# The attention mask of a hybrid block: written into the sigmoids' diagonal blocks by GpSimd, or added to the scores by VectorE

## The chip, the cores and the metric

The kernel runs on one core of one Trainium2 chip. The metric is the device time of one execution in microseconds (us); the median of three runs stands for a kernel. Every duration below comes from one profiled execution of the kernel before.

## The reference, cut to what matters

The whole block is a norm of x, ten projections, a stick-breaking attention of 8 heads, a retention of 4 heads, gates, and an output projection. Only the attention is touched. For a query t and a key s < t its weight is the sigmoid of the score times the product of (1 - sigmoid) over the keys between s and t; keys at and behind t count nothing:

```python
mask = kpos[None, :] < qpos[:, None]
log_keep = jnp.where(mask, jax.nn.log_sigmoid(-z), 0.0)
suffix = lax.cumsum(log_keep, axis=3, reverse=True) - log_keep
w = jnp.where(mask, jnp.exp(jax.nn.log_sigmoid(z) + suffix), 0.0)
return jnp.einsum('bhqk,bhkd->bhqd', w.astype(v.dtype), v)
```

The sequence has 512 tokens, a head is 128 wide, and the work is cut into blocks of 128 queries, so only the 128x128 block on the diagonal needs a mask.

## The kernel before, in words

**Dense stages.** Twenty-six dense products of 512x1024 by 1024x512 make up most of the work: the q/k groups qk0 to qk3 (two heads each), v0 and v1, the gates, the retention's projections, the two branch products and the final product. Each float32 operand is split into a high and a low part (`split`, L115 and L116: ScalarE copies the high part, VectorE subtracts to get the low one), and each product is three matmuls (`mm3`, L86). A dense stage takes four PSUM banks out of five (`ps_mm`) and walks over eight slices of 128 rows of the weights, which arrive by DMA in pairs and are split on the way.

**Side work.** Attention and retention are generators. After every two of a dense stage's tile products `work.step()` lets the generator at the front issue its next piece, so TensorE's order interleaves them. Matmuls, transposes and loads keep the order in which the program is written (`tc.keep_in_program_order`). The other engines' instructions are put in an order by a scheduler when the program is built, and each engine then works through its own list strictly in that order: one that waits holds up all behind it.

**A block of the attention** is a pair (head, query block), written (h, b) here. `scores` (L373 to L391) forms z in a side PSUM bank of TensorE, lets VectorE add the mask to the diagonal block (L382), lets ScalarE write keep = sigmoid(-z) (L385) and beta = sigmoid(z) (L386) into SBUF, and lets VectorE run the product of keep from the right as a scan (L387) and multiply it into beta (L391). `weights`, two blocks later, transposes beta on TensorE into a side bank pw (L89) and splits it into the pair wT (L115 on ScalarE, L116 on VectorE). `values`, three blocks after a head's last scores, multiplies all of wT with v into po (L86).

**GpSimd** has little to do. For each q/k group it raises the mean squares to -1/2 (L190, `rr`), multiplies this by the token norm (L302) and scales the four raw 128x512 tiles by it (L304, `qraw`). These are transposed much later by the generator `post`. When the groups qk0, qk1 and qk3 end, no scan of the attention is due; the group qk2 ends while heads 2 and 3 are in work, because qk2 follows directly on qk1.

The lines that the prediction speaks of:

```python
nc.vector.tensor_add(z[:, ts], z[:, ts], neg_mask)
nc.scalar.activation(keep[:, :n], z[:, :n], AF.Sigmoid, scale=-sc)
nc.scalar.activation(bt[:, :n], z[:, :n], AF.Sigmoid, scale=sc)
```

Of the kernel before, what the change touches and what calls it, by code (L numbers as in the profile page):

```python
# [7 lines left out]
F32 = mybir.dt.float32  # L8
F32R = mybir.dt.float32r
AF = mybir.ActivationFunctionType  # L10
ALU = mybir.AluOpType

P = 128
# [5 lines left out]
HD = 128  # L19
RH = 4  # L20
EPS = 1e-6
MASKED = -1e30

C_Q, C_K, C_V, C_G = 0, 1024, 2048, 3072
C_RQ, C_RK, C_RV, C_RG = 4096, 5120, 6144, 7168
# [42 lines left out]
def hybrid_block(ctx, tc, x, x_t, vecs, w_in, w_a, w_b, w_o, cos_t, sin_t, decay, out):  # L68
    nc = tc.nc
    PSUM = bass.MemoryType.PSUM  # L70

    const = ctx.enter_context(tc.tile_pool(name="const", bufs=1))
# [15 lines left out]
    def transpose(*a):  # L88
        tc.keep_in_program_order(nc.tensor.transpose(*a))  # L89

    def mm3(ps, a, b, first, last):

        matmul(ps, a[0], b[0], start=first, stop=False)
        matmul(ps, a[0], b[1], start=False, stop=False)
        matmul(ps, a[1], b[0], start=False, stop=last)

    def side_psum(name):
        return ps_a.tile([P, S], F32, tag="a", name=name)

    def T_tile(name, dtype=F32R):  # L100
        return big.tile([P, 4, S], dtype, tag="T", bufs=4, name=name)
# [4 lines left out]
    def O_pair(name):  # L106
        return [big.tile([P, S], F32R, tag="O", bufs=16, name=f"{name}_{q}") for q in range(2)]
# [3 lines left out]
    def tmp_tile(name):  # L111
        return tmp.tile([P, S], F32, tag="tmp", name=name)

    def split(hi, lo, src):
        nc.scalar.copy(hi, src)  # L115
        nc.vector.tensor_sub(lo, src, f32(hi))  # L116
# [54 lines left out]
    for j in range(N_IDLE):  # L171
# [1 line left out]

    ident = const.tile([P, P], F32, name="ident")
    make_identity(nc, ident)
    neg_mask = const.tile([P, P], F32, name="neg_mask")
    nc.gpsimd.memset(neg_mask, 0.0)
    nc.gpsimd.affine_select(
        out=neg_mask, in_=neg_mask, pattern=[[-1, P]], base=0, channel_multiplier=1,
        compare_op=ALU.is_gt, fill=MASKED,  # L180
    )
    for t in wT_pair:
        nc.vector.tensor_copy(t[:, NT - 1, (NT - 2) * P : (NT - 1) * P], zero.broadcast_to([P, P]))
    m_half = const.tile([P, M_ROOM], F32, name="m_half")[:, :16]
# [185 lines left out]
    def attention(heads, ready, v, gates):  # L370

        blocks = [(h, b) for h in heads for b in range(NT)]
        beta = {}  # L373

        def scores(h, b):
            hi, lo = qk_parts[h // 2]
            a, n = h % 2, (b + 1) * P
            ts = slice(b * P, n)
            z = side_psum(f"z{h}_{b}")
            m = max(n, 256)  # L380
            mm3(z[:, :m], (hi[:, a, ts], lo[:, a, ts]), (hi[:, 2 + a, :m], lo[:, 2 + a, :m]), True, True)
            nc.vector.tensor_add(z[:, ts], z[:, ts], neg_mask)  # L382
            bt = tmp.tile([P, S], F32, tag="beta", bufs=3, name=f"beta{h}_{b}")
            keep = tmp.tile([P, S], F32, tag="keep", bufs=2, name=f"keep{h}_{b}")
            nc.scalar.activation(keep[:, :n], z[:, :n], AF.Sigmoid, scale=-sc)  # L385
            nc.scalar.activation(bt[:, :n], z[:, :n], AF.Sigmoid, scale=sc)  # L386
            nc.vector.tensor_tensor_scan(  # L387
                keep[:, :n][:, ::-1], keep[:, :n][:, ::-1], zero.broadcast_to([P, n]), 1.0,
                op0=ALU.mult, op1=ALU.add,
            )  # L390
            nc.vector.tensor_mul(bt[:, : n - 1], bt[:, : n - 1], keep[:, 1:n])  # L391
            beta[h, b] = bt

        def weights(h, b):
            hi, lo = wT_pair
            bt = beta.pop((h, b))
            pw = side_psum(f"pw{h}_{b}").rearrange("p (i t) -> p i t", t=P)
            for i in range(b + 1):
                transpose(pw[:, i, :], bt[:, i * P : (i + 1) * P], ident)
            ts = slice(b * P, (b + 1) * P)  # L400
            split(hi[:, : b + 1, ts], lo[:, : b + 1, ts], pw[:, : b + 1, :])

        def values(h):
            hi, lo = wT_pair
            po = side_psum(f"po{h}")
            cs = slice((h % 4) * P, (h % 4 + 1) * P)
            vv = v()
            for i in range(NT):
                t0 = min(i, NT - 2) * P
                mm3(po[:, t0:], (vv[i][0][:, cs], vv[i][1][:, cs]), (hi[:, i, t0:], lo[:, i, t0:]),  # L410
                    i == 0, i == NT - 1)
            o = tmp_tile(f"oa{h}")
            nc.vector.tensor_mul(o, po, gates()[h % 4])
            oa[h] = O_pair(f"oa{h}")
            split(oa[h][0], oa[h][1], o)

        for n in range(len(blocks) + 3):
            if n < len(blocks):
                scores(*blocks[n])
                yield W_Z  # L420
            if n >= 3 and blocks[n - 3][1] == NT - 1:
                while not ready():
                    yield 1
                values(blocks[n - 3][0])
                yield W_Z
            if 2 <= n < len(blocks) + 2:
                weights(*blocks[n - 2])
                yield W_W
# [111 lines left out]
    for g in range(2):  # L540
        m = gate_group(f"ma{g}", C_MA + S * g, V_BM + 4 * g)
        ps = dense(f"pa{g}", branch_act(oa), w_a, ((S * g, S),), False)
        t = T_tile(f"pa{g}", F32)
# [26 lines left out]
    for g in range(2):  # L570
# [3 lines left out]
        for j in range(4):  # L574
            t = tmp_tile(f"mg{g}_{j}")
# [75 lines left out]
```

## Time and profile before

| what | value |
|---|---|
| median of three runs | 662.97 us (661.91 to 663.33) |
| the profiled execution | 663.5 us |
| its span, first to last instruction | 661.7 us |
| TensorE (PE) busy | 656.0 us, 99% of the span |
| VectorE (DVE), ScalarE (ACT), GpSimd (POOL) busy | 375.5, 260.4, 50.7 us |
| granted TensorE clock | full, mean 1.000 |

The span is the trace's own time; the execution's time has 1.8 us more around it. PEld is TensorE's loading of weights, which overlaps its matmuls. A row of a timeline gives the start in us, the duration in us, the engine, the line, the operation and its output and inputs; where the engine stood idle before, a bracket gives for how long and what ended the wait. Tile names there leave out buffer numbers and digits, so `keep`, `beta`, `z`, `pw` and `po` stand for all blocks and heads.

### The profile page before, as it was taken

What the parts mean: (1) busy time and instruction counts of PE and PEld (TensorE: products, weight loads), DVE (VectorE), ACT (ScalarE), POOL (GpSimd) and SP (SyncE); (2) the same over time, 40 slices, a digit from 0 to 9 for tenths busy, and PEclk for the clock granted to TensorE, in tenths of its full rate; (3) what the DMA queues carried; (4) which work ended last, traced back from release to release, by engine and by line L of the source; (5) the groups of instructions that cost most, each with busy time, mean ns of one, the idle gap of its engine ahead of it and who ended that gap; (6) DMA issues with size and microseconds to landing.
All of it is one profiled execution on the core that took longest, in us unless ns stands there. A gap on an engine that the chain in (4) does not pass through costs nothing.

```text
span 661.7 us, 7982 instructions
## 1 busy us (share of the span) xinstructions
PE 656.0 (99%) x3097; PEld 545.4 (82%) x3097; DVE 375.5 (57%) x560; ACT 260.4 (39%) x417; POOL 50.7 (8%) x50
## 2 busy tenths in 40 slices
PE   9999999999999999999999999999999999999997
PEld 6878888888888888888888888888888888888886
DVE  6356864587497477632344764844862953544632
ACT  5744534564354554522312342433433443422310
POOL 0051000340000400000000001001001001000000
PEclk9999999999999999999999999999999999999999
DMA  8533123322322323233223323222323322335441
GB/s 286 194 126 95 64 63 96 96 64 65 95 64 66 95 63 97 64 96 96 95 96 111 96 64 111 85 76 80 97 74 102 96 64 64 96 95 161 158 159 63
DMA packets 42182, 65.02 MB, mean 98 GB/s; under 512 B 2848, under 2 KB 19488, under 8 KB 42144
## 3 DMA queue, kind: packets, MB, share of 16 engines
q1 hardware_dynamic: 41424, 63.45, 30.9%
q10 hardware_dynamic: 720, 1.07, 0.4%
q8 instruction: 24, 0.39, 0.2%
q14 instruction: 14, 0.11, 0.1%
HBM read 62.41 MB, written 2.10 MB: 97 GB/s over the span
## 4 chain that ended last, share of the span: by engine, by line
PE 93%; DMA 2%; DVE 1%; ACT 1%; POOL 1%; issue 1%; SPq 0%; DVEq 0%; POOLq 0%
PE rqk_ps L86 13%; PE qk_ps L86 10%; PE sg_ps L86 7%; PE ma_ps L86 7%; PE rv_ps L86 7%; PE mb_ps L86 7%; PE rg_ps L86 7%; PE fin_ps L86 7%; PE pb_ps L86 7%; PE pa_ps L86 7%; PE v_ps L86 5%; PE po L86 2%; PE rz L86 2%; PE z L86 2%; PE ro L86 2%; PE pw L89 1%
## 5 line engine op out<-in xcount | busy, mean ns | idle before, releaser
L86 PE MATMUL qk_ps<-qk_hi,xT_hi 128*128 128x512 f32 x128 | 51.4, 410 | 0.0
L86 PE MATMUL rqk_ps<-xT_hi,rqk_hi 128*128 128x512 f32 x128 | 50.5, 394 | 0.0
L86 PE MATMUL rqk_ps<-xT_hi,rqk_lo 128*128 128x512 f32 x128 | 50.0, 390 | 0.0
L86 PE MATMUL rqk_ps<-xT_lo,rqk_hi 128*128 128x512 f32 x128 | 49.9, 390 | 0.0
L86 PE MATMUL qk_ps<-qk_hi,xT_lo 128*128 128x512 f32 x128 | 49.1, 391 | 0.0
L86 PE MATMUL qk_ps<-qk_lo,xT_hi 128*128 128x512 f32 x128 | 49.0, 391 | 0.0
L86 PE MATMUL pb_ps<-ob,pb_hi 128*128 128x512 f32 x128 | 39.4, 389 | 0.0
L86 PE MATMUL pa_ps<-oa,pa_hi 128*128 128x512 f32 x128 | 39.4, 389 | 0.0
L116 DVE TENSOR_TENSOR rqk_lo<-rqk_raw,rqk_hi 128x1024 fp32r<-128x1024 f32 x16 | 20.8, 1299 | 23.9 <-ACT rqk_hi L115 23.9
L387 DVE TENSOR_TENSOR_SCAN keep<-keep,zero 128x128 f32<-128x128 f32 (+3 forms) x32 | 27.1, 847 | 7.3 <-ACT keep L385 7.3
L86 PEld LDWEIGHTS qk_ps<-qk_hi,xT_hi 128*128 128x128 f32 x128 | 24.5, 192 | 5.3 <-ACT xT_hi L160 0.9
L86 PEld LDWEIGHTS qk_ps<-qk_hi,xT_lo 128*128 128x128 f32 x128 | 24.0, 188 | 5.2
L190 POOL TENSOR_TENSOR rrr<-ms,m_half 128x4 f32<-128x4 f32 x4 | 4.0, 1007 | 316.3 <-DVE ms L189 316.3
L86 PEld LDWEIGHTS rqk_ps<-xT_hi,rqk_lo 128*128 128x128 f32 x128 | 24.0, 188 | 5.1
L86 PEld LDWEIGHTS pa_ps<-oa,pa_hi 128*128 128x128 f32 x128 | 24.0, 188 | 5.0
L86 PEld LDWEIGHTS pb_ps<-ob,pb_hi 128*128 128x128 f32 x128 | 24.0, 188 | 5.0
L86 PEld LDWEIGHTS rqk_ps<-xT_hi,rqk_hi 128*128 128x128 f32 x128 | 24.1, 188 | 4.7
L86 PEld LDWEIGHTS rqk_ps<-xT_lo,rqk_hi 128*128 128x128 f32 x128 | 24.1, 188 | 4.6
L86 PEld LDWEIGHTS qk_ps<-qk_lo,xT_hi 128*128 128x128 f32 x128 | 24.3, 190 | 4.3
L115 ACT CAST rqk_hi<-rqk_raw 128x1024 fp32r<-128x1024 f32 x16 | 16.8, 1051 | 25.8 <-PE rqk_ps L86 16.5
L86 PE MATMUL v_ps<-v_hi,xT_hi 128*128 128x512 f32 x64 | 26.1, 408 | 0.0
L86 PE MATMUL sg_ps<-xT_hi,sg_hi 128*128 128x512 f32 x64 | 25.9, 404 | 0.0
(185 smaller groups left out, 1701.2 us busy)
## 6 DMA issues: line engine op xcount, KB each, us to landing
rqk_raw<-in_w_in SPq DMA_DIRECT2D x32, 256.0 KB, 2.9
qk_raw<-in_w_in SPq DMA_DIRECT2D x28, 256.0 KB, 3.0
v_raw<-in_w_in SPq DMA_DIRECT2D x8, 512.0 KB, 3.7
sg_raw<-in_w_in SPq DMA_DIRECT2D x8, 512.0 KB, 3.7
rv_raw<-in_w_in SPq DMA_DIRECT2D x8, 512.0 KB, 3.6
ma_raw<-in_w_in SPq DMA_DIRECT2D x8, 512.0 KB, 3.6
pa_raw<-in_w_a SPq DMA_DIRECT2D x8, 512.0 KB, 3.9
rg_raw<-in_w_in SPq DMA_DIRECT2D x8, 512.0 KB, 3.7
```

The costliest lines, as they stand in the source:

```text
L86: tc.keep_in_program_order(nc.tensor.matmul(*a, **k))
L89: tc.keep_in_program_order(nc.tensor.transpose(*a))
L115: nc.scalar.copy(hi, src)
L116: nc.vector.tensor_sub(lo, src, f32(hi))
L190: nc.gpsimd.tensor_tensor(dst, t[:, :width], m_half[:, :width], op=ALU.pow)
L387: nc.vector.tensor_tensor_scan(keep[:, :n][:, ::-1], keep[:, :n][:, ::-1], zero.broadcast_to([P, n]), 1.0, op0=ALU.mult, op1=ALU.add,)
```

## The change

The table of -1e30 (`neg_mask`) and the 32 additions of it to z in PSUM are gone. In their place GpSimd writes into the diagonal 128x128 block of each of the two sigmoids in SBUF: 1.0 into keep and 0.0 into beta where the key isn't earlier than the query. Each of the 32 blocks of the attention so has two selects (64 in all). The scan now waits for the select on keep, the product for the select on beta. Below the removed lines every line number is one lower up to L176, and from L178 on the function `earlier_keys` holds the selects (L178 for all 64); `scores` has its scan at L388 and its product at L392.

```diff
-MASKED = -1e30
...
-    neg_mask = const.tile([P, P], F32, name="neg_mask")
-    nc.gpsimd.memset(neg_mask, 0.0)
-    nc.gpsimd.affine_select(
-        out=neg_mask, in_=neg_mask, pattern=[[-1, P]], base=0, channel_multiplier=1,
-        compare_op=ALU.is_gt, fill=MASKED,
-    )
+
+    def earlier_keys(t, fill):
+
+        nc.gpsimd.affine_select(
+            out=t, in_=t, pattern=[[-1, P]], base=0, channel_multiplier=1, compare_op=ALU.is_gt, fill=fill,
+        )
...
-            nc.vector.tensor_add(z[:, ts], z[:, ts], neg_mask)
...
             nc.scalar.activation(keep[:, :n], z[:, :n], AF.Sigmoid, scale=-sc)
+            earlier_keys(keep[:, ts], 1.0)
             nc.scalar.activation(bt[:, :n], z[:, :n], AF.Sigmoid, scale=sc)
+            earlier_keys(bt[:, ts], 0.0)
```

TensorE's list and SyncE's are the same in both programs. Those of GpSimd, VectorE and ScalarE differ. In the listings the first digit of `keep_`, `beta_`, `z_` and `pw_` is the query block b, the last number is a buffer; the scan is listed as SCALAR_TENSOR_TENSOR.

GpSimd's list in the changed program, where the group qk2 ends; `keep_3_1294` is block (2,3), the last of head 2, and `keep_0_1325` is block (3,0), the first of head 3:

```order
L178 AFFINE_SELECT keep_3_1294<-keep_3_1294 128x128
L178 AFFINE_SELECT beta_3_1293<-beta_3_1293 128x128
L190 TENSOR_TENSOR rr_1253<-ms,m_half 128x16
L302 TENSOR_TENSOR rr_1253<-rr_1253,rx 128x16
L304 TENSOR_TENSOR qraw_0_1233<-qraw_0_1233,rr_1253 128x512
L304 TENSOR_TENSOR qraw_1_1235<-qraw_1_1235,rr_1253 128x512
L304 TENSOR_TENSOR qraw_2_1237<-qraw_2_1237,rr_1253 128x512
L304 TENSOR_TENSOR qraw_3_1239<-qraw_3_1239,rr_1253 128x512
L178 AFFINE_SELECT keep_0_1325<-keep_0_1325 128x128
L178 AFFINE_SELECT beta_0_1324<-beta_0_1324 128x128
L178 AFFINE_SELECT keep_1_1363<-keep_1_1363 128x128
```

Before, the six instructions of the group's norm stood alone here; now the selects of (3,0) and all that follow stand behind them, those of (2,3) ahead.

VectorE's list at the same place, before (`pw_3_1341` is the transposed block (2,3), `ms` what the group's norm waits for):

```order
L189 TENSOR_SCALAR ms<-ss_1204 128x16
L116 TENSOR_TENSOR v_lo_1368<-v_raw_1365,v_hi_1367 128x1024
L387 SCALAR_TENSOR_TENSOR keep_0_1295<-keep_0_1295,zero 128x128
L391 TENSOR_TENSOR beta_0_1294<-beta_0_1294,keep_0_1295 128x127
L116 TENSOR_TENSOR wT_77<-pw_2_1312,wT_76 128x3x128
L382 TENSOR_TENSOR z_1_1324<-z_1_1324,neg_mask 128x128
L387 SCALAR_TENSOR_TENSOR keep_1_1330<-keep_1_1330,zero 128x256
L391 TENSOR_TENSOR beta_1_1329<-beta_1_1329,keep_1_1330 128x255
L116 TENSOR_TENSOR wT_77<-pw_3_1341,wT_76 128x4x128
```

And in the changed program (`pw_3_1378` is block (2,3)):

```order
L189 TENSOR_SCALAR ms<-ss_1232 128x16
L115 TENSOR_TENSOR v_lo_1408<-v_raw_1405,v_hi_1407 128x1024
L115 TENSOR_TENSOR wT_77<-pw_2_1346,wT_76 128x3x128
L388 SCALAR_TENSOR_TENSOR keep_0_1325<-keep_0_1325,zero 128x128
L392 TENSOR_TENSOR beta_0_1324<-beta_0_1324,keep_0_1325 128x127
L388 SCALAR_TENSOR_TENSOR keep_1_1363<-keep_1_1363,zero 128x256
L392 TENSOR_TENSOR beta_1_1362<-beta_1_1362,keep_1_1363 128x255
L115 TENSOR_TENSOR wT_77<-pw_3_1378,wT_76 128x4x128
```

The subtraction for (2,3) stands behind two scans and two products as before, but these scans now wait for GpSimd.

VectorE's list where the gate group sg1 hands its PSUM banks to qk3, in the changed program (`sg_ps_1557` is the third of sg1's four banks, `keep_2_1744` is block (4,2)):

```order
L354 TENSOR_TENSOR sg_0_1759<-sg_0_1759,sg_s_1767 128x512
L388 SCALAR_TENSOR_TENSOR keep_2_1744<-keep_2_1744,zero 128x384
L349 TENSOR_TENSOR sg_2_1763<-sg_ps_1557,rb 128x512
L392 TENSOR_TENSOR beta_2_1743<-beta_2_1743,keep_2_1744 128x383
L115 TENSOR_TENSOR qk_lo_1855<-qk_raw_1851,qk_hi_1854 128x1024
L349 TENSOR_TENSOR sg_3_1765<-sg_ps_1558,rb 128x512
```

Before, the products that empty the third and fourth bank stood ahead of both the product with `sg_s` and the scan of (4,2); now the third stands behind them.

## Rows read from the trace of the kernel before

**Rows 1.** The page: busy time, share of the span and instructions of each engine.

```profile
PE 656.0 (99%) x3097; PEld 545.4 (82%) x3097; DVE 375.5 (57%) x560; ACT 260.4 (39%) x417; POOL 50.7 (8%) x50
```

**Rows 2.** Waits of TensorE: who for whom; us in total, times, longest.

```profile
PE pi L86 <- DVE idle L169: 1.2, 1, 1.2
PE pqk L89 <- POOL qraw L304: 0.4, 1, 0.4
```

**Rows 3.** The line L382: durations min/median/max in ns, and who waited for it.

```profile
L382 DVE TENSOR_TENSOR z<-z,neg_mask x32: 267/294/300, 59.8 to 265.5; 128x128 f32<-128x128 f32 x32
...
  ACT keep L385: 25.3, 18
```

**Rows 4.** Groups of GpSimd by form: busy us, mean ns of one.

```profile
L178 POOL TENSOR_SCALAR_AFFINE_SELECT neg_mask<-neg_mask 128x128 f32<-128x128 f32 x1 | 0.3, 287 | 0.0
```

**Rows 5.** Timeline of GpSimd, at the ends of the groups qk2 and qk3.

```profile
140.90 3.81 POOL L190 TENSOR_TENSOR rr<-ms,m_half 128x16 f32<-128x16 f32 x1 [18.35 <-DVE ms L189]
144.78 0.22 POOL L302 TENSOR_TENSOR rr<-rr,rx 128x16 f32<-128x16 f32 x1
145.08 5.08 POOL L304 TENSOR_TENSOR qraw<-qraw,rr 128x512 f32<-128x512 f32 x4
224.20 2.90 POOL L190 TENSOR_TENSOR rr<-ms,m_half 128x16 f32<-128x16 f32 x1 [74.04 <-DVE ms L189]
...
227.51 4.04 POOL L304 TENSOR_TENSOR qraw<-qraw,rr 128x512 f32<-128x512 f32 x4
```

**Rows 6.** Timeline of VectorE, 118 to 166 us.

```profile
140.66 0.16 DVE L189 TENSOR_SCALAR ms<-ss 128x16 f32<-128x16 f32 x1
140.73 1.22 DVE L116 TENSOR_TENSOR v_lo<-v_raw,v_hi 128x1024 fp32r<-128x1024 f32 x1
141.87 0.44 DVE L387 TENSOR_TENSOR_SCAN keep<-keep,zero 128x128 f32<-128x128 f32 x1
142.41 0.29 DVE L391 TENSOR_TENSOR beta<-beta,keep 128x127 f32<-128x127 f32 x1
142.62 0.55 DVE L116 TENSOR_TENSOR wT<-pw,wT 128x384 fp32r<-128x384 f32 x1
...
144.06 0.69 DVE L387 TENSOR_TENSOR_SCAN keep<-keep,zero 128x256 f32<-128x256 f32 x1 [0.51 <-ACT keep L385]
144.86 0.42 DVE L391 TENSOR_TENSOR beta<-beta,keep 128x255 f32<-128x255 f32 x1
145.68 0.69 DVE L116 TENSOR_TENSOR wT<-pw,wT 128x512 fp32r<-128x512 f32 x1 [0.40 <-ACT wT L115]
...
149.18 1.79 DVE L387 TENSOR_TENSOR_SCAN keep<-keep,zero 128x384 f32<-128x384 f32 x1
```

**Rows 7.** Timeline of TensorE, 143 to 168 us: the values of head 2.

```profile
148.19 0.63 PE L86 MATMUL po<-wT,v_hi 128*128 128x512 f32 x2
148.66 0.39 PE L86 MATMUL po<-wT,v_lo 128*128 128x512 f32 x1
```

**Rows 8.** Timeline of VectorE, 178 to 208 us: sg1 hands its banks to qk3.

```profile
188.44 1.28 DVE L349 TENSOR_TENSOR sg<-sg_ps,rb 128x512 f32<-128x512 f32 x2
...
190.78 0.95 DVE L387 TENSOR_TENSOR_SCAN keep<-keep,zero 128x384 f32<-128x384 f32 x1
191.65 0.67 DVE L354 TENSOR_TENSOR sg<-sg,sg_s 128x512 f32<-128x512 f32 x1
```

**Rows 9.** Timeline of TensorE, 180 to 200 us: qk3's first matmul in its fourth bank.

```profile
190.71 0.40 PE L86 MATMUL qk_ps<-qk_hi,xT_hi 128*128 128x512 f32 x1
```

**Rows 10.** Stretches: us, busy time of PE, PEld, DVE, ACT, POOL, granted PE clock, DMA.

```profile
657.80:661.70 3.90, 0.00 (x0) 0.00 (x0) 0.75 (x2) 0.00 (x0) 0.00 (x0) 1.00 0.38 134
```

**Rows 11.** Timeline of all engines from 0 to 12 us: TensorE's first matmuls.

```profile
1.19 4.02 PE L86 MATMUL pi<-idle 128*128 128x512 bf16 x9 [1.19 <-DVE idle L169]
...
5.24 2.06 PE L86 MATMUL qk_ps<-qk_hi,xT_hi 128*128 128x512 f32 x4
...
8.07 1.08 PE L86 MATMUL qk_ps<-qk_hi,xT_lo 128*128 128x512 f32 x4
```

## The prediction

> **What bounds the kernel now.** The page comes first: TensorE is busy for 656.0 of 661.7 us, so nothing that other engines save can show unless TensorE waits for it [rows 1]. Its waits come next, and there are two, 1.2 and 0.4 us, none of them on the attention [rows 2]. So the change can win next to nothing, and it costs whatever new wait it gives TensorE. The question is which of TensorE's operands come late, and that is read from the order of the lists and the timelines of the three engines behind it.
>
> **The parts that cost nothing.** The change takes 32 additions off VectorE, at 294 ns about 9.4 us, and ScalarE's waits for them, 25.3 us in 18 waits [rows 3]. Neither was on TensorE's path [rows 2], so I count 0. It adds 64 selects on GpSimd. One 128x128 float32 select took 287 ns at the start [rows 4], so they make 18.4 us on an engine that was busy for 50.7 us [rows 1]. The chain of a block is no longer for it: addition, sigmoid, scan becomes sigmoid, select, scan, with 287 ns in place of 294 and one handover more, on the product's side. A transpose comes two blocks after its scores, some 5 to 8 us later, and that room covers a handover. The memset and the select of the old table fall away at the start, where TensorE waits for VectorE and for DMA, again 0.
>
> **The part that costs: one queue.** GpSimd works its list in order. In the changed list the norm of group qk2 (one power, one small product, four scalings) stands between the selects of block (2,3) and those of block (3,0). In the trace of before this norm ran from 140.90 to 145.08 + 5.08 = 150.16 [rows 5], while VectorE ran the scan of (3,0) at 141.87 and that of (3,1) at 144.06 [rows 6]. Both scans now stand behind the norm, by way of their selects. Behind the scans on VectorE stands the subtraction that makes the low part of wT for block (2,3), at 145.68 before [rows 6]. TensorE needs this low part for its second matmul of head 2's values: the two first of them start at 148.19, the third at 148.66, so the second starts at about 148.42 [rows 7]. The transposes and scores ahead of it need nothing that is late.
>
> The new time of that subtraction, step by step:
> - `ms` ran at 140.66 [rows 6]. The addition ahead of it is gone, but the scan and the product of (2,3) ahead wait for selects. I take 0.3 us later, between 0.2 earlier and 0.5 later.
> - The power then starts at 140.90 + 0.3 = 141.2. It took 3.81 us here, where a subtraction of VectorE with two SBUF operands had begun just ahead of it [rows 5, 6], and 2.90 us where none had [rows 5]. The same subtraction still stands there in the changed list, so I take 3.81, with 2.90 as the low end. That is 145.0; the small product and two gaps of about 0.07 make 145.4.
> - The four scalings took 5.08 us beside VectorE's work and 4.04 us alone [rows 5]. VectorE now stands still, so 4.04: 149.4. High end 5.08.
> - The select on keep of (3,0) takes 0.29 [rows 4] and a handover 0.1, an estimate from the 0.08 between the end of `ms` and the start of the power: scan (3,0) starts at 149.8.
> - VectorE then runs 0.44 + 0.29 + 0.69 + 0.42 + 0.69 = 2.53 us [rows 6], with the gaps of about 0.1 ahead of each product set against the overlaps of the rest: 152.4 with nothing else in the way.
>
> Three more selects (beta of (3,0), both of (3,1)) run right then. The scan of 128x384 at 149.18 took 1.79 us while GpSimd was at its last scaling [rows 6], against 0.95 for the same form with GpSimd idle [rows 8]. So a GpSimd instruction can hold off a scan, and I allow the three selects 0 to 0.9 us (three times 0.29), and take 0.5: 152.9. TensorE loses 152.9 - 148.4 = **4.5 us**. The ends: all low values give 141.2 - 0.5 for the start, 0.9 less for the power and 0.5 less for the selects, so 2.6 us; all high ones 0.2 + 1.0 + 0.4 more, so 6.1 us.
>
> The Trainium skill has a rule on just this, in "SBUF — State Buffer", section "SBUF: two separate sides": a VectorE operation with two SBUF inputs and a GpSimd operation that reads SBUF exclude each other, the first one holding the pair of ports to its end. The trace agrees at the scan of 1.79 us. By the rule alone the three selects would cost from nothing to their full 0.9 us, according to who comes first, and the stall would be 4.0 to 4.9 us.
>
> Whether the stall is given back: TensorE has no gap later on to take it up [rows 1, 2], so all of it reaches the end. What is late next: the low part of v's last slices stands right behind the subtraction on VectorE and is ready at 154.1 (one more 1.22, as at 140.73 [rows 6]), while TensorE, itself 4.5 us late, needs it only about 7 us after the values; and ScalarE's keep of (3,2) waits for a buffer until the product of (3,0), which moves with the rest. I count 0 for both.
>
> **A second place.** Where sg1 ends, VectorE's product that empties the third bank ran first in a pair from 188.44 (1.28 us for two, so until 189.1) [rows 8], and TensorE wrote to that bank at 190.71 [rows 9]: 1.6 us of room. In the changed list a product with `sg_s`, 0.67, and the scan of 128x384, 0.95, stand ahead of it [rows 8]: 1.62 us, all of the room. The additions ahead that are gone give back up to 0.3, and the select and its handover ask for 0.4 to 0.9 (it may have to wait for that same product). I take **0.5 us**, between 0 and 0.9. Where sg0 hands its banks to qk1 the order of these products is kept, and where rv0 hands its banks on only one product moves behind a scan; I count 0 for both.
>
> **Sum.** 4.5 + 0.5 = 5.0 us. The profiled execution took 663.5, so it would take 668.5; the median of the runs is 0.5 lower, so I predict 662.97 + 5.0 = **668.0 us**.
>
> **The rivals.**
>
> *TensorE's clock falls in the stall.* 4.5 us without a matmul is longer than any gap in the trace of before. What the trace shows is a tail of 3.90 us after the last matmul with the granted clock still at 1.00, the level of 2.4 GHz [rows 10]. At the start, from idle, TensorE worked from 1.19, and four float32 matmuls took 2.06 us at 5.24 but 1.08 at 8.07 [rows 11]: half pace, that of 1.2 GHz, for some 6 us, 3.0 of them lost. If the clock falls here, I charge the same 3.0: 671.0 us. For it: the stall is longer than the tail that showed no fall. Against it: not by much. The Trainium skill, "TensorE: Matmul & The Clock Gate", Part 1, says that an idle TensorE is put back to half its clock and that activity releases it, which is this rival; no row of before shows a fall. I give it 0.2.
>
> *It is not slower.* This needs the subtraction for (2,3) before 148.4, so GpSimd's norm must end about 4.5 us sooner than I have it: if `ms` came that much earlier because VectorE is rid of its additions, or if the norm ran at half its time on a quieter port. Between 134 and 140 us, however, VectorE waits for ScalarE's squares rather than for time, and its additions there are three, 0.9 us in all. Then nothing stalls but at the second place, or not even there: 662.5 to 663.5 us, the low end if the two small waits of before [rows 2] go too. The point of decision is the order of GpSimd's list; a norm that ran behind the selects would give this case. I give it 0.1, a fifth of that for a real gain.
>
> *The ports are the cost.* If every select beside a two-operand subtraction of 1.22 us [rows 6] waits for its end, then the bank hand-overs at the ends of sg0, sg1 and rv0 each run late by up to that. Three times 1.2 beside 4.5 gives 671.1 us. For it speaks the scan of 1.79 [rows 6], against it that few of these subtractions stand beside a select there. I give it 0.08.
>
> **How the numbers follow.** The forecast has 0.62; its own range, by the ends above (2.6 to 6.1, and 0 to 0.9), is 665.6 to 670.0. The clock and the ports reach to about 671.5. The range 665.5 to 671.5 leaves out the third rival's tail and the case of no stall. About 0.2%, 1.3 us, is what a measurement of this kernel can tell from no change. Below 661.6 lies only the real gain, 0.02; between that and 664.3 the rest of no stall, 0.08; slower has 0.90.
>
> **What would show it.** In the changed profile: TensorE's waits with one of 4 to 5 us for VectorE's wT at the values of head 2, near 148 us; VectorE idle for some 6 to 7 us ahead of the scan of (3,0), released by GpSimd; on GpSimd four selects right behind the four scalings; a wait of about 0.5 us for `sg` near 195. TensorE's busy time stays at 656 us while the span grows. A granted clock below 1.00 near 150 us would show the first rival, no long wait at all the second, many waits of about 1 us the third. The prediction is wrong if `ms` comes much earlier, or if the selects take much more than 287 ns in place.

## The result and the profile after

The changed kernel takes 669.61 us (median of 6 runs, 667.79 to 670.34) against 663.02 us (6 runs, 661.91 to 663.65): a ratio of 1.0096, 95% interval 1.0079 to 1.0113. It is slower by 6.6 us. The profiled execution took 670.3 us, its span is 668.6.

The page of the changed kernel, its busy times, the granted clock in 40 slices, and the shares of the chain that ended last:

```profile
PE 658.6 (99%) x3097; PEld 546.5 (82%) x3097; DVE 369.0 (55%) x528; ACT 261.9 (39%) x417; POOL 79.7 (12%) x112
...
PEclk9999999997999999999999999999999999999999
...
PE 86%; POOL 4%; DMA 3%; DVE 3%; issue 2%; ACT 1%; SPq 0%; DVEq 0%; POOLq 0%; ACTq 0%
```

Against [rows 1] VectorE lost 6.5 us and GpSimd gained 29 us, neither of which matters by itself. What matters: GpSimd now holds 4% of the chain (1% before), and the clock has a dent in one slice. TensorE's waits in the changed kernel, to be held against [rows 2]:

```profile
PE po L85 <- DVE wT L115: 3.8, 1, 3.8
PE pi L85 <- DVE idle L168: 1.3, 1, 1.3
PE pqk L88 <- POOL qraw L304: 0.4, 1, 0.4
PE qk_ps L85 <- DVE qk_lo L115: 0.2, 1, 0.2
```

One long wait is new, on the low part of wT at `values`. The timeline of GpSimd leads up to it [rows 5]:

```profile
140.70 3.80 POOL L190 TENSOR_TENSOR rr<-ms,m_half 128x16 f32<-128x16 f32 x1 [2.03 <-DVE ms L189]
144.58 0.22 POOL L302 TENSOR_TENSOR rr<-rr,rx 128x16 f32<-128x16 f32 x1
144.88 4.04 POOL L304 TENSOR_TENSOR qraw<-qraw,rr 128x512 f32<-128x512 f32 x4
148.87 0.29 POOL L178 TENSOR_SCALAR_AFFINE_SELECT keep<-keep 128x128 f32<-128x128 f32 x1
149.11 0.29 POOL L178 TENSOR_SCALAR_AFFINE_SELECT beta<-beta 128x128 f32<-128x128 f32 x1
149.35 0.41 POOL L178 TENSOR_SCALAR_AFFINE_SELECT keep<-keep 128x128 f32<-128x128 f32 x1
149.72 0.29 POOL L178 TENSOR_SCALAR_AFFINE_SELECT beta<-beta 128x128 f32<-128x128 f32 x1
```

The norm of qk2 runs to 148.9 without a break, and four selects follow at once. They had been waiting for it: ScalarE had finished the keep of (3,0) at 140.23, while GpSimd stood idle for `ms`, and the beta of (3,1) at 143.49. VectorE's timeline at the same time [rows 6]:

```profile
140.44 0.17 DVE L189 TENSOR_SCALAR ms<-ss 128x16 f32<-128x16 f32 x1
...
149.19 0.48 DVE L388 TENSOR_TENSOR_SCAN keep<-keep,zero 128x128 f32<-128x128 f32 x1 [6.98 <-POOL keep L178]
149.78 0.37 DVE L392 TENSOR_TENSOR beta<-beta,keep 128x127 f32<-128x127 f32 x1
150.07 0.68 DVE L388 TENSOR_TENSOR_SCAN keep<-keep,zero 128x256 f32<-128x256 f32 x1
150.85 0.42 DVE L392 TENSOR_TENSOR beta<-beta,keep 128x255 f32<-128x255 f32 x1
151.20 0.68 DVE L115 TENSOR_TENSOR wT<-pw,wT 128x512 fp32r<-128x512 f32 x1
```

VectorE stands still for 6.98 us at the scan of (3,0), and the subtraction for (2,3), at 145.68 before, comes at 151.20. TensorE's timeline, from the transposes of (2,3) to the scores of (3,3), and its last matmul:

```profile
144.01 0.60 PE L88 MATMUL pw<-ident,beta 128*128 128x128 f32 x4
...
147.77 0.40 PE L85 MATMUL po<-wT,v_hi 128*128 128x512 f32 x1
151.93 0.79 PE L85 MATMUL po<-wT,v_hi 128*128 128x512 f32 x1 [3.77 <-DVE wT L115]
152.53 0.63 PE L85 MATMUL po<-wT,v_lo 128*128 128x512 f32 x1
...
159.42 0.39 PE L85 MATMUL z<-qk_hi 128*128 128x512 f32 x1
...
664.24 0.39 PE L85 MATMUL fin_ps<-fin_hi,mg_lo 128*128 128x512 f32 x1
```

The same four places in the kernel before (the second matmul of po there started at about 148.42 [rows 7]):

```profile
144.43 0.60 PE L89 MATMUL pw<-ident,beta 128*128 128x128 f32 x4
...
152.98 0.39 PE L86 MATMUL z<-qk_hi 128*128 128x512 f32 x1
...
657.39 0.39 PE L86 MATMUL fin_ps<-fin_hi,mg_lo 128*128 128x512 f32 x1
```

The difference between the two runs along these rows: -0.42 us at the transposes (the start went a little better), +3.51 at the second matmul of po, +6.44 at the scores of (3,3), +6.85 at the last matmul. So the stall cost 3.93 (3.51 and the 0.42 by which this run was ahead), and another 2.93 went in the 7.5 us behind it, where TensorE waits for nothing. There the float32 matmul takes 0.63 us in place of 0.39, and the next one follows after 0.43 in place of 0.23. The stretches of the changed kernel say why (us, busy time of PE, PEld, DVE, ACT, POOL, then the granted clock and DMA):

```profile
140.00:151.70 11.70, 8.17 (x42) 6.51 (x40) 4.47 (x10) 4.05 (x10) 9.74 (x12) 0.98 0.16 46
151.70:158.10 6.40, 6.17 (x19) 5.29 (x20) 4.12 (x6) 0.62 (x1) 0.05 (x1) 0.50 0.28 84
158.10:166.00 7.90, 7.90 (x41) 6.50 (x40) 4.14 (x6) 3.67 (x7) 1.45 (x2) 1.00 0.07 10
```

The granted clock fell to 0.50, the level of 1.2 GHz, near the end of the stall, stayed there until 158.1, and was full from then on. Of the remaining 0.4 us, 0.3 was lost at the second place; 0.1 is not located. Where qk3 takes sg1's third bank, VectorE's product that empties the bank came behind the scan,

```profile
194.92 0.68 DVE L354 TENSOR_TENSOR sg<-sg,sg_s 128x512 f32<-128x512 f32 x1
195.79 1.02 DVE L388 TENSOR_TENSOR_SCAN keep<-keep,zero 128x384 f32<-128x384 f32 x1 [0.19 <-POOL keep L178]
196.73 0.66 DVE L349 TENSOR_TENSOR sg<-sg_ps,rb 128x512 f32<-128x512 f32 x1
```

and TensorE wrote to it 0.3 us late (its matmuls follow each other by about 0.23):

```profile
196.91 0.40 PE L85 MATMUL qk_ps<-qk_hi,xT_lo 128*128 128x512 f32 x1
197.44 0.50 PE L85 MATMUL qk_ps<-qk_hi,xT_hi 128*128 128x512 f32 x1
```

### The profile page after: what moved, and what is told of

It is laid out like the page before. It is cut to its first block, busy times and chain, and to the rows that moved or that the text cites. A ratio compares the mean times of both kernels' runs of the same rounds, so it can differ in the third digit from the quotient of the medians.

```text
span 668.6 us, 8054 instructions
## 1 busy us (share of the span) xinstructions
PE 658.6 (99%) x3097; PEld 546.5 (82%) x3097; DVE 369.0 (55%) x528; ACT 261.9 (39%) x417; POOL 79.7 (12%) x112
## 4 chain that ended last, share of the span: by engine, by line
PE 86%; POOL 4%; DMA 3%; DVE 3%; issue 2%; ACT 1%; SPq 0%; DVEq 0%; POOLq 0%; ACTq 0%
PE rqk_ps L85 13%; PE sg_ps L85 7%; PE ma_ps L85 7%; PE rv_ps L85 7%; PE mb_ps L85 7%; PE rg_ps L85 7%; PE fin_ps L85 7%; PE pb_ps L85 7%; PE pa_ps L85 7%; PE qk_ps L85 6%; PE v_ps L85 3%; PE po L85 3%; PE rz L85 2%; PE ro L85 2%; PE z L85 2%
## 5 line engine op out<-in xcount | busy, mean ns | idle before, releaser
L388 DVE TENSOR_TENSOR_SCAN keep<-keep,zero 128x128 f32<-128x128 f32 (+3 forms) x32 | 27.8, 867 | 21.5 <-POOL keep L178 21.5
L178 POOL TENSOR_SCALAR_AFFINE_SELECT keep<-keep 128x128 f32<-128x128 f32 x32 | 15.2, 474 | 119.2 <-ACT keep L384 116.9
```

The costliest lines, as they stand in the source:

```text
L178: nc.gpsimd.affine_select(out=t, in_=t, pattern=[[-1, P]], base=0, channel_multiplier=1, compare_op=ALU.is_gt, fill=fill,)
L388: nc.vector.tensor_tensor_scan(keep[:, :n][:, ::-1], keep[:, :n][:, ::-1], zero.broadcast_to([P, n]), 1.0, op0=ALU.mult, op1=ALU.add,)
```

## The experiments

The theory after the result: one queue on GpSimd makes a stall of 3.9 us, and the stall lets TensorE's clock fall, which costs 2.9 more. The main rival: the 64 selects cost by themselves, by the ports that VectorE and GpSimd share or by the longer chain of each block. The first four runs shared one set of runs of the kernel before (662.87 us), the last two another (663.09).

**Fill the stall with work.** Seventeen idle matmuls go into po, whose first real matmul overwrites it:

```diff
             po = side_psum(f"po{h}")
             cs = slice((h % 4) * P, (h % 4 + 1) * P)
+            for j in range(17 if h == 2 else 0):
+                matmul(po, idle[:, :P], idle, start=True, stop=True)
```

> The changed kernel with 17 idle 128x512 bf16 matmuls into po ahead of head 2's values, some 3.7 us of TensorE's time where it stood still for 3.8. Theory (one queue on GpSimd stalls TensorE, and the stall lets its clock fall): the matmuls fill the stall, the granted clock stays at 1.00, and only the stall is left: 663.0 + 3.8 + 0.3 for the second place = 667.1 us, although work was added. Rival (the slow matmuls behind the stall come from late operands or contention, not from standing still): 669.6 as the change, and as much as 3.7 more if the stall isn't where the matmuls are.

Measured: 666.88 us, ratio 1.0065 (1.0052 to 1.0077), 2.7 us less than the changed kernel with 17 matmuls more. TensorE's timeline there:

```profile
147.78 3.84 PE L85 MATMUL po<-idle 128*128 128x512 bf16 x17
151.28 1.16 PE L85 MATMUL po<-wT,v_hi 128*128 128x512 f32 x2
152.27 0.39 PE L85 MATMUL po<-wT,v_lo 128*128 128x512 f32 x1
```

and its stretches behind the place:

```profile
150.00:155.00 5.00, 4.92 (x26) 3.50 (x25) 4.79 (x8) 0.87 (x2) 0.66 (x3) 1.00 0.19 29
155.00:160.00 5.00, 5.00 (x25) 4.06 (x24) 2.39 (x5) 3.03 (x6) 1.44 (x2) 1.00 0.22 84
```

The clock stays full and the matmuls behind take 0.39 us. The operands come as late as before: the low part of wT is ready at 151.88 in both kernels. The scores of (3,3) start at 156.59, 2.83 us ahead of the changed kernel. So the 2.9 us were the clock, and it fell because TensorE stood still.

**Undo the queue alone.** The norm of qk2 goes behind head 3's selects; all 64 selects stay. A few instructions need their written order for it:

```diff
+    def hold(i, fixed):
+        if fixed:
+            tc.keep_in_program_order(i)
...
-        nc.gpsimd.affine_select(
+        hold(nc.gpsimd.affine_select(
             out=t, in_=t, pattern=[[-1, P]], base=0, channel_multiplier=1, compare_op=ALU.is_gt, fill=fill,
-        )
+        ), fixed)
...
             beta[h, b] = bt
+            if (h, b) == (3, 3):
+                later.pop()()
...
+        if p == 2:
+            later.append(norm)
+        else:
+            norm()
```

Here `norm` holds the lines of qk_group from `rr` to the scalings, and `fixed` is set for the selects of head 3 and for this norm's power.

> The changed kernel with GpSimd's norm of group qk2 behind the selects of head 3 (the selects of head 3 and that norm's power keep the order in which they are written, and the norm is written behind block (3,3)). All 64 selects stay. Theory (the queue): no wait of TensorE for wT, the clock at 1.00, 663.0 + 0.3 = 663.3 us. Rival (the ports that VectorE and GpSimd share, or the longer chain of each block): the selects cost as before, 668 to 669.6 us.

Measured: 663.30 us (11 runs), ratio 1.0007 (0.9999 to 1.0016): not to be told from the kernel before. TensorE's waits in full:

```profile
PE pi L85 <- DVE idle L168: 1.3, 1, 1.3
```

VectorE runs the scan of (3,0) and the subtraction for (2,3) where they were before [rows 6]:

```profile
140.72 0.51 DVE L399 TENSOR_TENSOR_SCAN keep<-keep,zero 128x128 f32<-128x128 f32 x1
...
144.31 0.69 DVE L115 TENSOR_TENSOR wT<-pw,wT 128x512 fp32r<-128x512 f32 x1 [0.34 <-ACT wT L114]
```

The norm now starts at 154.83 and nobody waits for it. That rules the main rival out: with all 64 selects in place the loss is gone. It also shows that the change has nothing to win that could be measured, since VectorE's 32 additions are gone here too.

**A shorter and a longer norm.** Of the four scalings of group qk2 two, or all, are left out, or two are done twice (the same line, with other values in the range):

```diff
-        for tb in range(NT):
+        for tb in range(2 if p == 2 else NT):
             nc.gpsimd.tensor_tensor(
```

> The changed kernel without two of the four scalings of group qk2 (heads 4 and 5 so work on unscaled q and k in half of their tokens). GpSimd's norm is 2.0 us shorter. Theory: the wait at head 2's values shrinks by as much, 3.8 to 1.8 us, perhaps in two pieces (VectorE's list has the subtraction for (2,2) behind the scan of (3,0)), too short for the clock to fall: 663.0 + 1.8 + 0.3 = 665.1 us, clock 1.000. If the clock falls with a stall of 1.8 us too, 668; if the loss is in proportion to the norm, 666.3.

> The changed kernel without all four scalings of group qk2 (heads 4 and 5 work on unscaled q and k). The norm is 4.0 us shorter. Theory: the subtraction for (2,3) is ready 0.3 to 0.8 us ahead of TensorE, at most 0.5 us are lost on the bank of (2,2): 663.3 to 663.8 us. Rival (ports or chain): 668 or more.

> The changed kernel with two of the four scalings of group qk2 done twice (heads 4 and 5 have these tiles scaled twice). GpSimd's norm is 2.0 us longer. Theory: the wait at head 2's values grows from 3.8 to 5.8 us and the clock falls as before, 669.6 + 2.0 = 671.6 us; up to 1.5 more if it is down for longer. Rival (ports or chain): 669.6.

Measured without all four: 663.77 us, ratio 1.0022 (1.0013 to 1.0031), with a wait of 0.55 us on the bank of (2,2): as expected. With two done twice TensorE's wait is

```profile
PE po L85 <- DVE wT L115: 5.8, 1, 5.8
```

so the stall grew by the 2.0 us of the two scalings; the time is 670.74 us, ratio 1.0121 (1.0106 to 1.0136), 7.65 above its kernel before in place of the 8.6 expected. Its profiled execution was the longest of four, 672.13; the others took 670.5 to 670.8. TensorE's timeline in the profiled one, at the second matmul of po and the scores of (3,3):

```profile
153.76 0.79 PE L85 MATMUL po<-wT,v_hi 128*128 128x512 f32 x1 [5.76 <-DVE wT L115]
...
161.20 0.39 PE L85 MATMUL z<-qk_hi 128*128 128x512 f32 x1
```

That is 7.44 us from the one to the other, against 7.49 in the changed kernel and 4.56 before. So the stall and the clock's 2.9 us were as forecast here; what the other three runs saved stands in no trace.

Without two of them the time is 667.59 us (665.48 to 667.94), ratio 1.0067 (1.0053 to 1.0080), 2.5 above the 665.1 that I expected. TensorE's long wait there is

```profile
PE z L85 <- DVE wT L115: 2.7, 1, 2.7
```

and its stretches (columns as above):

```profile
145.00:150.00 5.00, 2.33 (x9) 1.71 (x8) 3.01 (x7) 1.84 (x3) 2.83 (x7) 0.88 0.00 2
150.00:155.00 5.00, 5.00 (x23) 4.21 (x22) 3.35 (x4) 0.39 (x2) 1.20 (x2) 0.78 0.36 108
155.00:160.00 5.00, 5.00 (x25) 4.04 (x24) 2.17 (x4) 2.75 (x6) 1.44 (x2) 1.00 0.01 3
```

Two things were wrong in that expectation. The wait is 2.7 us, because in this program's order TensorE stops earlier, at a bank held by the subtraction for (2,2), which VectorE runs at 147.66, behind the scan of (3,0). And the clock fell here with a stop of 2.7 us: the stretch from 149 to 150 us has 0.50, though TensorE had started again at 148.26. It cost 1.7 us: from there to the scores of (3,3) are 8.39 us, against 6.72 before. Of its five runs the one with the highest mean clock, 0.999, took 665.48 us, about what the stop alone would give (662.87 + 2.7 = 665.6); the other four, at 0.996 to 0.997, took 666.6 to 667.9.

**Half of the selects.** The selects on beta are left out, so later keys keep a weight:

```diff
-            earlier_keys(bt[:, ts], 0.0)
```

> The changed kernel without the 32 selects on beta (its diagonal blocks keep the later keys). Theory (the queue): the wait for the norm is the same, only the selects beside the first scans are fewer: 669.2 to 669.6 us, the wait at head 2's values 3.4 to 3.8 us. Rival (each select costs, by the ports or the chain): half of the loss goes, 666.3 us.

Measured: 670.59 us, ratio 1.0117 (1.0100 to 1.0134), no lower than the changed kernel; the wait at head 2's values is 3.6 us. The rival wanted half of the loss gone. The number of selects doesn't matter, the one place in the queue does. The time is about 1 us above what I expected; the granted clock of these runs, 0.993 to 0.997, is that of the changed kernel, and the two intervals overlap. The total is the weaker witness here: in the profiled execution, 669.63 us, the clock cost 1.7 us (6.23 from the second matmul of po to the scores of (3,3), against 4.56 before), and the span ends 5.4 us after the last matmul starts, where the profiled executions of all other kernels have 4.3. The wait says it: 3.6 us with half of the selects, 3.8 with all.

## Why the prediction was right, and where it was off

The direction, the place and the way were right, point by point:
- `ms`: forecast 0.3 us later; it ran at 140.44 against 140.66, and in this run all had started 0.42 earlier, so 0.2 later.
- The power: 3.81 forecast, 3.80 measured; the scalings 4.04 and 4.04. Both rows of before held: the subtraction with two SBUF operands still began ahead of the power, and VectorE stood still beside the scalings. Where the norm was put behind head 3's selects no such subtraction began ahead, and the power took 2.90.
- Select to scan: I took a handover of 0.1 behind a select of 0.29. The scan started 0.32 behind the select's start, so this was 0.07 too long.
- From the scan's start to the subtraction's end: 3.03 us forecast (2.53, and 0.5 for three selects in the way), 2.69 measured (149.19 to 151.88). The selects cost 0.16, and without those on beta the same work took 2.54 (148.86 to 151.40). **This term was too large**, and together with the start and the handover it made the stall 4.5 where 3.9 was measured.
- The second place: 0.5 forecast, 0.3 measured.
- What costs nothing: undoing the queue gave the kernel before to within its interval, with the additions gone and the selects in. Right for the time, but the sizes were off: the selects take 31.4 us in place of 18.4 (15.2 on keep and 16.2 on beta), and VectorE lost 6.5 us in place of 9.4.
- Two readings of the rows of before were wrong, without consequence. Between 134 and 140 us VectorE has one addition and waits 0.15 us for squares; the three additions lie between 131 and 141. And from a block's scores to its transpose are 5.4 to 15.1 us in heads 0 to 3, not 5 to 8.
- TensorE's busy time was to stay at 656 us. It is 658.6: the slow matmuls behind the stall.

**The step that failed is the choice between the forecast and its first rival.** I gave the fall of the clock 0.2, because the tail of 3.90 us had shown none [rows 10]. It fell in the profiled execution, and none of the six runs has a mean clock above 0.997, where those of the kernel before have 0.999 or 1.000. The price that I had set, 3.0 us from the start of the trace [rows 11], came out at 2.93. With the stall as I had it and this rival the time would have been 671.0. In the profiled execution it is 663.5 + 3.9 + 2.9 + 0.4 less 0.4 for the better start, the 670.3 that it took. The median fell between the two cases, 1.6 us above the forecast and inside the range. That it lies even inside the forecast's own 665.6 to 670.0 is luck: that range had the ends of the stall and of the second place in it, and nothing for the clock.

The tail was a bad witness: what it shows is that a stop of 3.9 us need not bring the clock down before the trace ends, not that it doesn't. In the changed kernel's own trace it does: the last matmul ends at 664.6, and from 667 us on the granted clock is 0.50.

The Trainium skill's page "TensorE: Matmul & The Clock Gate", Part 1, says that an idle TensorE is throttled and activity releases it; the run with the filled stall agrees, 1.00 with the matmuls and 0.50 without. The Trainium skill's rule in "SBUF — State Buffer", section "SBUF: two separate sides", by which the first of two such operations holds the ports to its end, is borne out by single rows, not by the total. Select durations in the changed kernel:

```profile
L178 POOL TENSOR_SCALAR_AFFINE_SELECT keep<-keep x32: 292/294/1289, 60.8 to 273.1; 128x128 f32<-128x128 f32 x32
L178 POOL TENSOR_SCALAR_AFFINE_SELECT beta<-beta x32: 287/293/1272, 62.1 to 273.6; 128x128 f32<-128x128 f32 x32
```

The median is [rows 4]'s 0.29 us, the longest took 1.3; fourteen of the 64 took 0.84 or more. One on beta at 137.51 took 1.16 us and so ended at 138.67, with the scan of 512 that had begun at 137.35 and took 1.23. TensorE's waits name none of these.

## What to carry to other kernels

Before work goes to an idle engine, look at what already stands in that engine's list at the same time, and who waits behind the instruction that will now wait for it: 51 us of work in 662 did not make GpSimd free at the one moment that counted. Where a stall of TensorE can't be avoided, count the clock into its price, or give TensorE something to do meanwhile: adding 17 useless matmuls made this kernel 2.7 us faster. And when an order is made by a scheduler, a change that touches no order by hand can still move it; the cure here was to write the norm further down and to hold the order of nine instructions.

## What the runs showed of the hardware that I had not expected

- The granted clock fell with a stop of 2.7 us in one kernel, while 3.9 us at the end of another's trace showed no fall. When it fell varied as well. With the longer norm TensorE stopped at 148.0, and the stretch from 152 to 153 us still has 0.99. In the runs without two scalings and without the selects on beta the clock fell only after TensorE was back at work: in the latter it was back at 151.46, and the stretch from 151 to 152 still has 1.00, the one from 153 to 154 has 0.50.
- What a fall cost didn't go with the length of the stop. In the profiled executions it was 2.9 us with stops of 3.8 and 5.8 us, and 1.7 with stops of 2.7 and 3.6. What decides between the two isn't shown.
- The times of one program spread more where the clock falls: the changed kernel's six runs lie between 667.8 and 670.3 us, a spread of 2.5 where the kernel before has 1.7. The mean clock alone doesn't order them: four of the six have 0.997, and they took 667.8 to 669.9 us.
